# One decay matrix per unit in a chunked DeltaNet layer: the strength moved to the other side of the triangular system, and the second layer-start work held back

## The chip, the core and the metric

The kernel runs on one core of a Trainium2 chip. The core has a matrix engine (TensorE, PE in the profile; its weight loads are PEld), three engines for elementwise work (VectorE, DVE; ScalarE, ACT; GpSimd, POOL) and a queue that issues DMAs (SyncE, SP). Each engine works through its own instructions in order and waits on semaphores for the others. The metric is the time of one execution in microseconds, as a median over several runs.

## The reference

Two layers over a sequence of 1024 tokens and 1024 channels. Layer 0 is a gated DeltaNet (16 value heads, 8 key heads of 128), layer 1 is a softmax attention with a forget bias. Before each layer stands an RMSNorm whose result is scaled and shifted by a projection of a conditioning vector c (adaLN), and the layer's output is multiplied by a gate that comes from the same projection. The change touches layer 0. Its core, cut to what matters:

```python
# per head, per chunk of tokens; g = cumulative log decay inside the chunk
decay = exp(where(lower, g[:, None] - g[None, :], -inf))
kb, vb = k * beta[:, None], v * beta[:, None]
L = where(strict, (kb @ k.T) * decay, 0)
T = inverse(I + L)                      # unit lower triangular
u = T @ vb
w = T @ (kb * exp(g)[:, None])
attn = (q @ k.T) * decay
# scan over the chunks
v_new = u - w @ state
o     = (q * exp(g)[:, None]) @ state + attn @ v_new
state = state * exp(g_last) + (k * exp(g_last - g)[:, None]).T @ v_new
```

q and k are normalised per head (l2norm) after a short causal convolution. The strength beta, and with k unnormalised also the square of the reciprocal norm of k, multiplies the rows of L. The same matrix can be had with the strength as a diagonal on the other side: with B the diagonal of strengths and N the strictly lower part of (k k^T) * decay, (I + B N)^-1 B = B (I + N B)^-1.

## The kernel before

The kernel uses chunks of 128 tokens, two halves of 512 tokens (four chunks each), and units: a unit is one key head with its two value heads in one half, so there are 16 units, 8 per half. Matrix products of the projections run as three products of numbers split in a high and a low part (`mm3`), so each weight tile is cast to `whi` on ACT and its rest `wlo` is taken on DVE (`split`, L323 and L326). In the first half each split tile is written to a cache in HBM (`wc`, L719); in the second half it is read back (`proj_src`, L398).

For each unit run these stages, each of which is a generator:

- `proj_conv`: the projections for k, q and two v tiles, with the convolution on DVE (L743).
- `prepk`: builds a decay matrix `d1` (`decay`, L828 to 854), brings k to token order (`to_tokens`, evicted as `ktok`, L902), takes the reciprocal norm on POOL (`rk`, L867), the strengths `un`, `wn`, `weg`, and multiplies k k^T by strength and decay into `lm` (L884).
- `invert_blocks`: writes the diagonal blocks of `lm` to HBM (`lb`), reads them back spread over partitions (`lr`), inverts the 16 by 16 blocks on DVE (`xi`, L1065 and L1069), writes them (`rb`) and reads them into `rmat` (L1082). `invert_merge` joins blocks on PE with small matmuls (`su`, `tr`), copies on ACT and transposes on DVE (`tmat`).
- `prepv`: brings v to token order (`vtok`, L902) and multiplies it by `un` on POOL (L918).
- `prep2`: builds a second decay matrix `d2`, `qd` = q times exp(g) (L929) and the attention weights `am` (L937).
- `chain`: four steps over the chunks, with `xp` (L957), `vn` on ACT (L970), `ve` on DVE (L971), the state and the outputs `og`.
- `finish`: norm, gate and split of the outputs of both heads, then two DMAs of 512 KB to `og_d` and `ogl_d` (L1037).

A decay matrix starts with `gb`, a 512 KB DMA that spreads two rows of g (in `g_d`, written by `gates`, L696) over all partitions (L834); `affine_select` on POOL writes g with the triangle filled (L840), and eight `exp` on ACT finish it (L852). `gb` has one buffer, `d1` and `d2` have two each. Banks of PSUM are rings: `tr` has two, so a third transpose group waits until the first was evicted.

At the start `start_norm` normalises the first half and computes the scale and shift of layer 0 from eight weight tiles each (accumulated on DVE at L555 for the first six, `KPE`, and on PE with one-column matmuls for the rest). `ada_all` computes everything else of adaLN in 16 strips of 256 columns: 128 DMAs of 128 KB (`oraw`, L265), each followed by one DVE operation (L270, L272). Before its first load it touches the three `oraw` buffers with a copy of `scol[0]` (L1177), so that the loads can't start before that column exists. `next_norm` prepares the second half's input.

What sets the order: the order on PE is written by a planner (`Flow`). Each stage is a generator that yields the time (the `Y_` constants) until its next part is due; the planner always runs the due stage of highest priority, and the projections (later the output projection) are the filler at the lowest. The order on DVE, ACT, POOL and SP is made by the framework's scheduler from dependencies, priorities and its own estimates. So PE never takes a later matmul ahead of one that waits, and SP never issues a later DMA ahead of one that waits.

After layer 0 the output projection (`out_proj_a`) streams its weights twice; then come layer 1 and its output projection, which the change doesn't touch.

Of the kernel before, what the change touches and what calls it, by code (L numbers as in the profile page):

```python
# [37 lines left out]
Y_PK = 1200  # L38
# [4 lines left out]
Y_P2 = 4000  # L43
# [10 lines left out]
Y_F1 = 800  # L54
Y_F2 = 2550
# [25 lines left out]
KPE = 6  # L81
# [100 lines left out]
def tile_trunk(  # L182
# [209 lines left out]
    def proj_src(src, key, again):  # L392
        def load():
            if again:
# [10 lines left out]
            return [(hi, lo, key)]  # L405
# [85 lines left out]
    with ExitStack() as sa:  # L491
# [34 lines left out]
        def start_norm():  # L526
            xsT = [at([P, HALF], n, b) for n, b in (("k", KQ), ("k", KQ), ("k", KQ), ("q", 2), ("q", 2))]
            xsT += [at([P, HALF], "ktok", 3) for _ in range(3)]
            for t in range(CPH):
                xt = at([P, D], *(("vtok", 3), ("qd", 2))[t // 2])  # L530
                nc.sync.dma_start(xt, x[t * P : (t + 1) * P, :])
                for d in norm_tile(xt, at([P, D], "ogt", 1), lambda k, p, t=t: nc.scalar.copy(
                    xsT[k][:, t * P : (t + 1) * P], p)):
                    flow.t += d
            tags = [("d1", 2), ("og", 2), ("zg", ZG), ("d1", 2), ("og", 2), ("zg", ZG), ("gb", 1)]
# [10 lines left out]
            for n in range(2):  # L546
                ps = banks[n]
                acc = at([P, D], "d2", 2)
                for k in range(KT):
# [8 lines left out]
                    for s, c, on in ((acc, ones[:, 0:1], k == KPE), (w, cond[:, k : k + 1], k >= KPE)):  # L558
                        for j in range(KT if on else 0):
                            mm(  # L560
                                ps[:, j : j + 1], s[:, j * P : (j + 1) * P], c,
                                start=s is acc and j == 0, stop=k == KT - 1 and j == KT - 1,
# [29 lines left out]
        def norm_tile(xt, jk, evac):  # L592
            rs = rms_rows(xt, jk, at)
# [13 lines left out]
        def next_norm():  # L607
            yield from hold(lambda: done["kqv"] >= 2)
            for t in range(CPH):
                tok = CPH * P + t * P  # L610
                xt = at([P, D], "nx", 1)
                nc.sync.dma_start(xt, x[tok : tok + P, :])
                yield 4000
                hf = at([P, KT, P], "nh", 1)

                def evac(k, p):
                    nc.vector.tensor_scalar(
                        hf[:, k], p, gcol[0][:, k : k + 1], scol[0][:, k : k + 1],
                        op0=ALU.mult, op1=ALU.add,
                    )  # L620

                yield from norm_tile(xt, hf.rearrange("p k t -> p (k t)"), evac)
                yield 3000
                nc.sync.dma_start(
                    h1_d[:, :, t * P : (t + 1) * P].rearrange("k p t -> p k t"), hf
                )
# [12 lines left out]
        def gates(h, gt):  # L639
# [44 lines left out]
            nc.scalar.activation(ex, ex, AF.Exp)  # L684
            ngc = at([P, CPH, 16], "g_ngc", 2)
# [12 lines left out]
            gt.update(col=col, ex=ex, ngc=ngc, beta=beta, g_d=g_d)  # L698
# [132 lines left out]
        def decay(t, name):  # L831
            gb = at([P, 2, HALF], "gb", 1)
# [5 lines left out]
            dv = at([P, 2 * CPH, P], name, 2)  # L838
            low = name == "d1"
            nc.gpsimd.affine_select(  # L840
                out=dv, in_=gb.rearrange("p j (c t) -> p (j c) t", t=P),
                compare_op=ALU.is_gt if low else ALU.is_ge, fill=BIG if low else -BIG, base=0,
                pattern=[[0, 2 * CPH], [-1 if low else 1, P]], channel_multiplier=1 if low else -1,
            )
            bias = t["gt"]["col" if low else "ngc"]
            yield Y_DG
            for j in range(2):
                for c in range(CPH):
# [4 lines left out]
                        dv[:, u], dv[:, u], AF.Exp, scale=-1.0 if low else 1.0, bias=bias[:, c, hd : hd + 1]  # L853
                    )
            return gb, dv

        def prepk(t):
            g, gt, kf = t["g"], t["gt"], t["k"]
            _, d1v = yield from decay(t, "d1")
            yield Y_PK  # L860
            t["ktok"] = ktok = at([P, CPH, P], "ktok", 3)
            t["ss"] = ss = at([P, 2, CPH], "gss", 3)
            yield from to_tokens(kf, ktok, ss[:, 0])
            yield Y_PS
            rk = at([P, CPH], "rk", 2)
            nc.vector.tensor_scalar(rk, ss[:, 0], EPS, None, op0=ALU.add)
            nc.gpsimd.tensor_tensor(rk, rk, mhalf[:, 0:CPH], op=ALU.pow)  # L867
            rkb = bc(rk, 2, 2)
            t["un"] = un = at([P, CPH, 2], "un", 3)
            t["wn"] = wn = at([P, CPH, 2], "wn", 2)  # L870
            t["weg"] = weg = at([P, CPH, 2], "weg", 3)
            nc.vector.tensor_tensor(un, gt["beta"][:, :, 2 * g : 2 * g + 2], rkb, op=ALU.mult)
            nc.vector.tensor_tensor(wn, un, rkb, op=ALU.mult)
            nc.vector.scalar_tensor_tensor(
# [944 lines left out]
```

## Time and profile before

| what | value |
|---|---|
| median of 3 runs | 2058.69 us (2054.26 to 2058.92) |
| the profiled execution | 2063.72 us, its span 2062.0 us |
| PE, DVE, ACT, POOL busy | 1853.8, 1364.0, 1033.1, 476.4 us |
| instructions | 36440 |
| mean granted TensorE clock | 0.952 |
| DMA | 322.55 MB, 156 GB/s over the span |

The span goes from the first to the last instruction. Busy times of PE are of pipelined matmuls and don't say that PE is at its peak. A row of the waits names who waited, for whom, the total in us, how often, and the longest; a row of the timeline starts with the time in us from the start of the span and the duration, and ends with the number of equal instructions in the row and, in brackets, the idle time ahead and what ended it. In the table of stretches each engine has its busy time in us with the number of instructions, then follow the granted clock, the share of the DMA engines and GB/s.

### The profile page before, as it was taken

What the parts mean: (1) busy time and instruction counts of PE and PEld (TensorE: products, weight loads), DVE (VectorE), ACT (ScalarE), POOL (GpSimd) and SP (SyncE); (2) the same over time, 40 slices, a digit from 0 to 9 for tenths busy, and PEclk for the clock granted to TensorE, in tenths of its full rate; (3) what the DMA queues carried; (4) which work ended last, traced back from release to release, by engine and by line L of the source; (5) the groups of instructions that cost most, each with busy time, mean ns of one, the idle gap of its engine ahead of it and who ended that gap; (6) DMA issues with size and microseconds to landing.
All of it is one profiled execution on the core that took longest, in us unless ns stands there. A gap on an engine that the chain in (4) does not pass through costs nothing.

```text
span 2062.0 us, 36440 instructions
## 1 busy us (share of the span) xinstructions
PE 1853.8 (90%) x12972; PEld 1549.9 (75%) x12972; DVE 1364.0 (66%) x3310; ACT 1033.1 (50%) x2678; POOL 476.4 (23%) x518
## 2 busy tenths in 40 slices
PE   5867898988998889989989788999999999999898
PEld 5655676767776677778778566879889889889676
DVE  5867888778767567665666476537656566666664
ACT  3554565554545345554444343336555565555631
POOL 2021221211213122212101231421231331331222
PEclk7888999999999999999999999999999999999999
DMA  8767676667655545454459998310211110111522
GB/s 320 255 194 219 192 248 205 202 211 238 198 164 178 154 133 176 128 177 140 145 172 311 323 317 274 108 53 27 67 45 33 57 57 32 57 59 40 170 84 95
DMA packets 238166, 322.55 MB, mean 156 GB/s; under 512 B 103896, under 2 KB 156656, under 8 KB 237984
## 3 DMA queue, kind: packets, MB, share of 16 engines
q1 hardware_dynamic: 237984, 320.22, 48.4%
q8 instruction: 102, 1.67, 0.3%
q14 instruction: 80, 0.66, 0.1%
HBM read 235.34 MB, written 84.81 MB: 155 GB/s over the span
## 4 chain that ended last, share of the span: by engine, by line
PE 57%; DMA 16%; DVE 14%; ACT 5%; issue 3%; POOL 3%; SPq 2%; DVEq 0%; POOLq 0%; ACTq 0%
PE mm L127 36%; PE lg L127 5%; PE pt L131 3%; PE oT L127 3%; DMA oraw<-in_ada_w_dram 3%; PE su L127 2%; PE tr L131 2%; PE co L127 2%; DMA rmat<-rb 2%; DVE wlo L326 2%; DMA ohi<-og_d 2%; PE ch L127 2%; DVE cv_y L743 1%; DMA gb<-g_d 1%; DVE xtmp L1065 1%
## 5 line engine op out<-in xcount | busy, mean ns | idle before, releaser
L127 PE MATMUL mm<-ht_h,whi 128*128 128x512 f32 x784 | 352.1, 449 | 8.8 <-DVE olo L299 6.2
L127 PE MATMUL mm<-ht_l,whi 128*128 128x512 f32 x784 | 317.2, 405 | 5.7 <-DVE ht_l L582 5.7
L127 PE MATMUL mm<-ht_h,wlo 128*128 128x512 f32 x784 | 317.5, 405 | 0.9 <-POOL wlo L326 0.9
L127 PE MATMUL mm<-whi,h_h 128*128 128x384 f32 x512 | 187.3, 366 | 1.7 <-ACT whi L323 1.7
L127 PEld LDWEIGHTS mm<-ht_h,whi 128*128 128x128 f32 x784 | 155.0, 198 | 40.3 <-DVE olo L299 6.7
L127 PEld LDWEIGHTS mm<-ht_h,wlo 128*128 128x128 f32 x784 | 153.4, 196 | 37.0 <-POOL wlo L326 1.3
L127 PEld LDWEIGHTS mm<-ht_l,whi 128*128 128x128 f32 x784 | 154.9, 198 | 32.6 <-DVE ht_l L582 6.9
L127 PE MATMUL mm<-wlo,h_h 128*128 128x384 f32 x512 | 174.1, 340 | 2.7 <-POOL wlo L326 2.7
L743 DVE SCALAR_TENSOR_TENSOR cv_y<-cv_t,conv_h,cv_y 128x512 f32<-128x512 f32 x192 | 146.5, 764 | 42.7 <-ACT cv_y L735 40.4
L127 PE MATMUL mm<-whi,h_l 128*128 128x384 f32 x512 | 173.6, 339 | 0.0
L1559 DVE TENSOR_TENSOR ptl<-pt,pth 128x512 fp32r<-128x512 f32 x192 | 106.3, 555 | 85.0 <-ACT pth L1558 83.3
L1558 ACT CAST pth<-pt 128x512 fp32r<-128x512 f32 x192 | 91.3, 477 | 130.5 <-PE pt L131 129.4
L1402 POOL TENSOR_TENSOR rs<-ss,mhalf 128x4 f32<-128x4 f32 x64 | 64.5, 1007 | 313.3 <-DVE ss L1400 310.6
L1523 ACT ACTIVATE lg<-lg,mx 128x896 f32<-128x896 f32 (+7 forms) x128 | 99.5, 777 | 54.1 <-DVE mx L1515 49.8
L326 DVE TENSOR_TENSOR wlo<-ht_h,whi 128x512 fp32r<-128x512 f32 x124 | 92.3, 785 | 49.9 <-ACT whi L323 44.0
L323 ACT CAST whi<-ht_h 128x512 fp32r<-128x512 f32 x124 | 70.5, 619 | 91.4 <-DMA ht_h<-in_wa_o_dram 37.4
L127 PEld LDWEIGHTS mm<-wlo,h_h 128*128 128x128 f32 x512 | 97.9, 191 | 6.3 <-POOL wlo L326 4.4
L127 PEld LDWEIGHTS mm<-whi,h_h 128*128 128x128 f32 x512 | 98.5, 192 | 4.4 <-ACT whi L323 2.0
L127 PE MATMUL mm<-h_h,whi 128*128 128x512 f32 x240 | 100.4, 419 | 0.6 <-DVE wlo L1658 0.3
L131 PE MATMUL pt<-ident,lg 128*128 128x128 f32 (+1 forms) x584 | 96.6, 275 | 2.8 <-ACT lg L1523 2.8
L127 PEld LDWEIGHTS mm<-whi,h_l 128*128 128x128 f32 x512 | 97.2, 190 | 0.0
L127 PE MATMUL mm<-h_h,wlo 128*128 128x512 f32 x240 | 94.8, 395 | 0.0
(356 smaller groups left out, 4660.6 us busy)
## 6 DMA issues: line engine op xcount, KB each, us to landing
ht_h<-in_wa_o_dram SPq DMA_DIRECT2D x62, 512.0 KB
wc<-whi SPq DMA_DIRECT2D x48, 512.0 KB
wc<-wlo SPq DMA_DIRECT2D x48, 512.0 KB
wlo<-wc SPq DMA_DIRECT2D x48, 512.0 KB
whi<-wc SPq DMA_DIRECT2D x48, 512.0 KB
wlo<-in_wa_c_dram SPq DMA_DIRECT2D x32, 512.0 KB
oraw<-in_ada_w_dram SPq DMA_DIRECT2D x128, 128.0 KB
gb<-g_d SPq DMA_DIRECT2D x32, 512.0 KB
```

The costliest lines, as they stand in the source:

```text
L127: self.nc.tensor.matmul(out, lhsT, rhs, start=start, stop=stop)
L131: self.nc.tensor.transpose(out, src, ident)
L323: nc.scalar.copy(hi, src)
L326: (lo_eng or nc.gpsimd).tensor_tensor(lo, src, hi.bitcast(F32), op=ALU.subtract)
L743: nc.vector.scalar_tensor_tensor(y, raw[:, j : j + HALF], w[:, j : j + 1], y, op0=ALU.mult, op1=ALU.add)
L1065: nc.vector.tensor_tensor(tv, bc(lr[:, j + 1 :, j], 1, m), xi[:, 0:m, j : j + 1].broadcast_to([P, m, n]), op=ALU.mult,)
L1402: nc.gpsimd.tensor_tensor(rs, ss, mhalf[:, 0:4], op=ALU.pow)
L1523: nc.scalar.activation(lg, lg, AF.Exp, scale=-1.0, bias=mx[:, hh : hh + 1], accum_out=sums[:, tt : tt + 1],)
L1558: nc.scalar.copy(ph_[:, cs], pp[:, cs])
L1559: nc.vector.tensor_tensor(pl_[:, cs], pp[:, cs], ph_[:, cs].bitcast(F32), op=ALU.subtract)
```

## The change

1. **One decay matrix.** `decay` is called once per unit, in `prepk`, after k was brought to token order; it builds `d2` alone (three buffers instead of two), with `gb` in two buffers instead of one, and also takes the exponential of `gb` that `qd` needs. `prep2` uses `gb` and `d2` as they are. `lm` is now k k^T times strength times `d2` and so the transposed matrix, with the strength on the other index; it has its own tile. The inverse and its merges take the operands in the other order (32 by 16 instead of 16 by 16 in one of the first two products); the first product reads `tmat` and the second `rmat`.
2. **The strength on the other side.** `un` and `weg` are gone. v is scaled by `irk`, the norm of k, when ACT evicts it, two chunks of both heads at a time (POOL's product, L918, is gone), `xp` uses a negated exp(g), and the strength `wn` multiplies the solution: `vn` becomes two ACT operations of 128 columns with a scale instead of one copy of 256, and `ve` multiplies by `wex`.
3. **Held until the gates.** The three copies in `ada_all` and a new one in `next_norm` read `ngc` of the first gates instead of `scol[0]`, so that the strips' loads and the second half's first input wait for the gates.
4. **Start.** `KPE` goes from 6 to 7, and the `gb` tag of `start_norm`'s weight tiles has two buffers.
5. **Cache.** The first three tiles (`KC`) aren't written to the cache; in the second half they are loaded and split again.
6. **Finish and next norm.** `finish` works head by head with one buffer each for `ogt`, `ogh`, `ogl` of 512 columns, and stores with four DMAs of 256 KB; `next_norm` works in halves.
7. Some `Y_` constants of the planner change.

The diff, cut:

```diff
-KPE = 6
+KPE = 7
+KC = 3
...
-            if again:
+            if again and key >= KC:
...
-            tags = [("d1", 2), ("og", 2), ("zg", ZG), ("d1", 2), ("og", 2), ("zg", ZG), ("gb", 1)]
+            tags = [("d1", 2), ("og", 2), ("zg", ZG), ("d1", 2), ("og", 2), ("zg", ZG), ("gb", 2)]
...
                 xt = at([P, D], "nx", 1)
+                if t == 0:
+                    nc.vector.tensor_copy(xt[:, 0:KT], ts[0]["gt"]["ngc"][:, 0, 0:KT])
                 nc.sync.dma_start(xt, x[tok : tok + P, :])
...
-                if k == 2 and key is not None:
+                if k == 2 and key is not None and key >= KC:
...
-        def decay(t, name):
-            gb = at([P, 2, HALF], "gb", 1)
+        def decay(t):
+            gb = at([P, 2, HALF], "gb", 2)
...
-            dv = at([P, 2 * CPH, P], name, 2)
-            low = name == "d1"
+            dv = at([P, 2 * CPH, P], "d2", 3)
...
+            for j in range(2):
+                yield 2 * Y_DX
+                nc.scalar.activation(gb[:, j], gb[:, j], AF.Exp)
             return gb, dv
...
-            _, d1v = yield from decay(t, "d1")
-            yield Y_PK
             t["ktok"] = ktok = at([P, CPH, P], "ktok", 3)
             t["ss"] = ss = at([P, 2, CPH], "gss", 3)
+            yield Y_PT
             yield from to_tokens(kf, ktok, ss[:, 0])
-            yield Y_PS
+            t["gb"], t["d2"] = yield from decay(t)
...
+            nc.vector.tensor_tensor(irk, irk, rk, op=ALU.mult)
...
+            t["lm"] = lm = at([P, 2 * CPH, P], "d1", 2)
...
                     nc.vector.scalar_tensor_tensor(
-                        d1v[:, u], mq[:, c * P : (c + 1) * P], wn[:, c, j : j + 1], d1v[:, u],
+                        lm[:, u], mq[:, c * P : (c + 1) * P], wn[:, c, j : j + 1], t["d2"][:, u],
...
-            for j in range(2):
+            for c0 in range(0, CPH, 2):
                 yield Y_PT
-                yield from to_tokens(vt[:, j], vtok[:, :, j], None)
...
+                    nc.scalar.activation(
+                        vtok[:, c].rearrange("p j f -> p (j f)"), tr[:, o : o + 2 * P], AF.Copy,
+                        scale=t["irk"][:, c : c + 1],
+                    )
...
-            for c in range(CPH):
-                nc.gpsimd.tensor_tensor(vtok[:, c], vtok[:, c], bc(t["un"][:, c], 2, P), op=ALU.mult)
...
-            gb, d2 = yield from decay(t, "d2")
+            gb, d2 = t["gb"], t["d2"]
...
-                nc.scalar.copy(vn, p1[:, 256:512])
+                for j in range(2):
+                    nc.scalar.activation(
+                        vn[:, j * P : (j + 1) * P], p1[:, 256 + j * P : 256 + (j + 1) * P], AF.Copy,
+                        scale=wn[:, c, j : j + 1],
+                    )
...
-            ogh = at([P, 2, HALF], "ogh", 1, F32R)
-            ogl = at([P, 2, HALF], "ogl", 1, F32R)
-            for j in range(2):
-                split(ogh[:, j], ogl[:, j], ogt[:, j], lo_eng=nc.vector)
-                yield 1500
-            for v, d in ((ogh, og_d), (ogl, ogl_d)):
...
+                yield Y_F1
+                ogh, ogl = at([P, HALF], "ogh", 1, F32R), at([P, HALF], "ogl", 1, F32R)
+                split(ogh, ogl, ogt, lo_eng=nc.vector)
+                yield Y_F2
+                for v, d in ((ogh, og_d), (ogl, ogl_d)):
+                    nc.sync.dma_start(d[2 * g + j, :, h * HALF : (h + 1) * HALF], v.bitcast(F32))
...
                 for b in range(4):
-                    o = 32 * b
-                    mm(
-                        pbk[b][o : o + 16, us], lm[sls[b], u, o : o + 16], r[sls[b], u, o + 16 : o + 32],
-                        start=True, stop=True,
-                    )
+                    h16 = slice(32 * b, 32 * b + 16)
+                    mm(pbk[b][sls[b], us], lm[h16, u, sls[b]], tms[b][0:16, u, 0:16], start=True, stop=True)
...
             for _ in range(3):
-                nc.vector.tensor_copy(xt_([P, 2 * P], "oraw", 3)[:, 0:KT], scol[0])
+                nc.vector.tensor_copy(xt_([P, 2 * P], "oraw", 3)[:, 0:KT], ts[0]["gt"]["ngc"][:, 0, 0:KT])
```

**Where it moves instructions.** On SP, at the start of layer 0, around the write of the first gates' g (`g_d`). `oraw` are the strips' weight loads, `wc` the writes to the cache, `wlo` loads of projection weights, `gb` the spread of g. Before:

```order
L265 DMA oraw<-in_ada_w_dram 128x256 x3
L401 DMA wlo<-in_wa_c_dram 128x1024
L265 DMA oraw<-in_ada_w_dram 128x256 x21
L401 DMA wlo<-in_wa_c_dram 128x1024
L265 DMA oraw<-in_ada_w_dram 128x256
```

```order
L696 DMA g_d<-cv_t 16x512
L401 DMA wlo<-in_wa_z_dram 128x1024
L834 DMA gb<-g_d 128x1024
L719 DMA wc_1190<-whi 128x1024
L719 DMA wc_1191<-wlo 128x1024
L834 DMA gb<-g_d 128x1024
L401 DMA wlo<-in_wa_z_dram 128x1024
L719 DMA wc_1253<-whi 128x1024
L719 DMA wc_1254<-wlo 128x1024
L834 DMA gb<-g_d 128x1024 x2
```

and with the change:

```order
L739 DMA wc_1002<-whi 128x1024
L739 DMA wc_1003<-wlo 128x1024
L266 DMA oraw<-in_ada_w_dram 128x256 x3
L716 DMA g_d<-cv_t 16x512
L627 DMA nx<-in_x_dram 128x1024
L402 DMA wlo<-in_wa_z_dram 128x1024
L266 DMA oraw<-in_ada_w_dram 128x256
L854 DMA gb<-g_d 128x1024 x2
L739 DMA wc_1065<-whi 128x1024
L266 DMA oraw<-in_ada_w_dram 128x256 x2
```

Of the strips' 128 loads 35 stood ahead of `g_d`, now 3; the first two units' `gb` now stand next to each other.

On ACT, the first two units. `d_757` and `d_881` are the `d1` of units 0 and 1, `d_872` the `d2` of unit 0; with the change `d_772` and `d_949` are the `d2` of units 0 and 1. Before:

```order
L852 ACTIVATE d_757<-d_757,g_gc 128x128 x8
L898 ACTIVATE sqt,gss<-tr 128x128
L747 ACTIVATE cv_t<-cv_y 128x512
L852 ACTIVATE d_872<-d_872,g_ngc 128x128 x3
L928 ACTIVATE gb<-gb 128x512
L852 ACTIVATE d_872<-d_872,g_ngc 128x128
L928 ACTIVATE gb<-gb 128x512
L852 ACTIVATE d_872<-d_872,g_ngc 128x128 x4
L898 ACTIVATE sqt,gss<-tr 128x128 x2
L902 COPY ktok<-tr 128x512
L898 ACTIVATE sqt,gss<-tr 128x128 x4
L902 COPY vtok<-tr 128x4x128 x2
```

and with the change:

```order
L870 ACTIVATE d_772<-d_772,g_ngc 128x128 x4
L919 ACTIVATE sqt,gss<-tr 128x128
L870 ACTIVATE d_949<-d_949,g_ngc 128x128 x3
L875 ACTIVATE gb<-gb 128x512 x2
L870 ACTIVATE d_949<-d_949,g_ngc 128x128 x5
L767 ACTIVATE cv_t<-cv_y 128x512
L919 ACTIVATE sqt,gss<-tr 128x128 x3
L923 COPY ktok<-tr 128x512
L919 ACTIVATE sqt,gss<-tr 128x128 x4
L940 ACTIVATE vtok<-tr,irk 128x256 x4
```

The eviction `ktok` of unit 0 went ahead of all exponentials; the `ktok` shown is unit 1's, and the first `vtok` now stands behind the exponentials of both units.

On ACT again, the casts `ogh` of one unit's outputs, with the change:

```order
L754 COPY cv_t<-mm 128x512
L755 ACTIVATE cv_y<-mm,conv_h 128x512
L1000 ACTIVATE vn<-ch,wn 128x128 x2
L324 CAST ogh<-ogt 128x512 x2
L1029 ACTIVATE sqt,so<-co 128x128 x2
L1032 COPY og<-co 128x256
```

The second of the two casts writes the buffer that the DMA of the first reads; in the order before the two heads had a buffer each.

More of the change, by code (lines that the diff above doesn't have):

```diff
@@ L37 @@
 Y_PT = 650
-Y_PK = 1200
+Y_PK = 1000
 Y_DG = 2500
@@ L561, in start_norm @@
                                 ps[:, j : j + 1], s[:, j * P : (j + 1) * P], c,
-                                start=s is acc and j == 0, stop=k == KT - 1 and j == KT - 1,
+                                start=s is acc and j == 0, stop=s is w and k == KT - 1 and j == KT - 1,
                             )
@@ L592, in norm_tile @@
         def norm_tile(xt, jk, evac):
-            rs = rms_rows(xt, jk, at)
+            if jk is None:
+                ss = at([P, 2], "ln_s2", 2)
+                for c in range(2):
+                    nc.scalar.activation(
+                        at([P, HALF], "nh", 1), xt[:, c * HALF : c * HALF + HALF], AF.Square,
+                        accum_out=ss[:, c : c + 1],
+                    )
+                nc.vector.tensor_tensor(ss[:, 0:1], ss[:, 0:1], ss[:, 1:2], op=ALU.add)
+                nc.vector.tensor_scalar(ss[:, 0:1], ss[:, 0:1], 1.0 / D, EPS, op0=ALU.mult, op1=ALU.add)
+                rs = at([P, 1], "ln_rs", 2)
+                nc.gpsimd.tensor_tensor(rs, ss[:, 0:1], mhalf[:, 0:1], op=ALU.pow)
+            else:
+                rs = rms_rows(xt, jk, at)
             nc.vector.tensor_scalar(xt, xt, rs, None, op0=ALU.mult)
@@ L697, in gates @@
             done["gates"] = h + 1
-            gt.update(col=col, ex=ex, ngc=ngc, beta=beta, g_d=g_d)
+            gt.update(neg=neg, ex=ex, ngc=ngc, beta=beta, g_d=g_d)
         def z_after(i):
@@ L909, in prepv @@
             vtok = at([P, CPH, 2, P], "vtok", 3)
-            for j in range(2):
+            for c0 in range(0, CPH, 2):
                 yield Y_PT
-                yield from to_tokens(vt[:, j], vtok[:, :, j], None)
+                tr = yield from pst("tr", 2)
+                for c in (c0, c0 + 1):
+                    for j in range(2):
+                        o = (2 * (c - c0) + j) * P
+                        tr_(tr[:, o : o + P], vt[:, j, c], ident)
+                for c in (c0, c0 + 1):
+                    o = 2 * (c - c0) * P
+                    nc.scalar.activation(
+                        vtok[:, c].rearrange("p j f -> p (j f)"), tr[:, o : o + 2 * P], AF.Copy,
+                        scale=t["irk"][:, c : c + 1],
+                    )
+                flow.free(tr, R_T)
             done["tr"] += 1
@@ L969, in chain @@
                 ve = at([P, 2, P], "ve", 2)
-                nc.scalar.copy(vn, p1[:, 256:512])
+                for j in range(2):
+                    nc.scalar.activation(
+                        vn[:, j * P : (j + 1) * P], p1[:, 256 + j * P : 256 + (j + 1) * P], AF.Copy,
+                        scale=wn[:, c, j : j + 1],
+                    )
                 nc.vector.tensor_tensor(
                     ve, p1[:, 256:512].rearrange("p (j f) -> p j f", f=P),
-                    bc(ex[:, 0, c, 2 * g : 2 * g + 2], 2, P), op=ALU.mult,
+                    bc(wex[:, c], 2, P), op=ALU.mult,
                 )
@@ L1164, in invert_merge @@
                 mm(
[L1165 removed]
+                    p3[0:64, u * 64 : u * 64 + 64], pq[64:128, u], r[64:128, u, 64:128],
+                    start=True, stop=True,
                 )
```

103 lines of the change are left out of this document (50 added, 53 removed).

## The prediction

> **What bounds the kernel now.** I read the table of stretches first, cut where the trace changes its character: start, the first units, the first half of layer 0, the change of halves, the second half, the output projection, layer 1.
>
> ```profile
> 0.00:64.00 64.00, 33.72 (x140) 29.89 (x141) 40.03 (x75) 24.91 (x62) 14.35 (x30) 0.66 0.79 281
> 64.00:200.00 136.00, 103.44 (x745) 82.99 (x745) 97.02 (x253) 67.98 (x174) 27.00 (x44) 0.88 0.74 237
> 200.00:600.00 400.00, 357.17 (x3198) 289.24 (x3198) 315.08 (x793) 219.28 (x655) 88.90 (x116) 0.95 0.66 208
> 600.00:700.00 100.00, 81.91 (x549) 67.14 (x547) 66.42 (x179) 45.21 (x140) 22.51 (x29) 0.90 0.54 164
> 700.00:1065.00 365.00, 340.40 (x3133) 279.17 (x3132) 240.30 (x618) 183.08 (x576) 68.16 (x86) 0.98 0.48 144
> 1065.00:1310.00 245.00, 215.46 (x1121) 171.44 (x1120) 151.05 (x261) 102.41 (x216) 54.99 (x38) 0.96 0.88 296
> ```
>
> The columns behind the length are busy us of PE, PEld, DVE, ACT, POOL, then the granted clock. Nearly all of the change lies in the 1001 us from 64 to 1065. PE is busy there for 882.9 us and idle for 118.1; the change hardly alters PE's work, so that idle time, and the 64 us of the start, is what can be won. It isn't even: PE is idle for 32.6 of 136 us among the first units and for 18.1 of 100 at the change of halves, but for 7% of the stretch from 700. The waits of PE from 64 to 1065 name the reasons:
>
> ```profile
> PE su L127 <- DMA rmat<-rb: 22.1, 4, 10.3
> PE tr L131 <- ACT vtok L902: 17.8, 5, 8.5
> PE co L127 <- DVE ve L971: 15.4, 13, 2.9
> PE ch L127 <- DVE xp L957: 14.3, 7, 4.4
> PE tr L131 <- ACT ktok L902: 12.5, 1, 12.5
> PE co L127 <- ACT vn L970: 7.8, 8, 3.0
> PE mm L127 <- DVE olo L299: 6.2, 1, 6.2
> ```
>
> Four single stalls (10.3 on `rmat`, 8.5 on `vtok`, 12.5 on `ktok`, 6.2 on `olo`) make 37.5 us and the other three on `rmat` 11.8; the rest are many short waits inside the chain.
>
> **The change part by part.** All of the sum is made against the profiled execution (2063.72 us, 5.0 over the median of 2058.69) and then taken from the median.
>
> Start. The timeline of PE:
>
> ```profile
> 39.48 3.57 PE L127 MATMUL mm<-ones,d 128*128 128x1 f32 x16 [6.22 <-DVE d L555]
> 52.43 0.80 PE L127 MATMUL mm<-ht_h,whi 128*128 128x512 f32 x1 [2.55 <-ACT ht_h L577]
> 60.55 0.80 PE L127 MATMUL mm<-ht_l,whi 128*128 128x512 f32 x1 [4.18 <-DVE ht_l L582]
> ```
>
> With `KPE` 7 one group of eight one-column products per pass goes, of the form of the first row (-3.5), and DVE does one more accumulation at L555, some 1.3. The strips' loads no longer compete with the last weight tiles, nor do two cache writes and one early x tile of 512 KB each: at the stretch's 281 GB/s these 1.5 MB and the first 0.8 MB of strips are 8 us of DMA, of which I count half as ahead of the last tile (-4). On DVE the strips' operations stand between those that make `ht_l`; without them the 4.18 us go mostly (-3). About **-9**, from -12 to -5.
>
> First stall. The same view of SP, ACT and PE, and of POOL and DVE for later:
>
> ```profile
> 95.76 0.32 SPq L696 DMA_DIRECT2D g_d<-cv_t  x1
> 104.74 0.32 SPq L834 DMA_DIRECT2D gb<-g_d  x1
> 103.26 1.46 POOL L840 TENSOR_SCALAR_AFFINE_SELECT d<-gb 128x1024 f32<-128x1024 f32 x1 [4.13 <-DMA gb<-g_d]
> 110.23 1.10 POOL L840 TENSOR_SCALAR_AFFINE_SELECT d<-gb 128x1024 f32<-128x1024 f32 x1 [4.93 <-DMA gb<-g_d]
> 104.75 2.44 ACT L852 ACTIVATE d<-d,g_gc 128x128 f32<-128x128 f32 x8
> 115.40 0.58 ACT L902 COPY ktok<-tr 128x512 f32<-128x512 f32 x1
> 116.03 1.11 PE L131 MATMUL tr<-ident,vt 128*128 128x128 f32 x4 [12.48 <-ACT ktok L902]
> ```
>
> PE waits for a bank that holds `ktok`, which in ACT's order stands behind the exponentials of two matrices, made from two `gb` loads that share one buffer: the second (5.5 us from issue to POOL) starts after POOL has read the first. From `g_d` to `ktok` pass 20 us. Afterwards the first `ktok` stands ahead of the exponentials, but PE's third transpose group then needs unit 1's `ktok`, which stands behind two units' exponentials. The two loads overlap: 7.5 us to the first matrix on POOL, 2 more for the second load, POOL 1.2, then 16 exponentials at 2.44 for 8 and four of `gb`, taken like the copy of that size at 0.58, make 7.2: 18. So the stall only shrinks: **-2.5** (0 to -12.5).
>
> Second and third stall.
>
> ```profile
> 134.00 0.79 PE L127 MATMUL mm<-ht_h,whi 128*128 128x512 f32 x1 [6.25 <-DVE olo L299]
> 191.25 3.56 DMA rb<-xi
> 194.94 1.78 SPq L1082 DMA_DIRECT2D rmat<-rb  x4
> L1092 DVE STREAM_TRANSPOSE tmat<-rmat 32x256 f32<-32x256 f32 x64 | 27.9, 436 | 30.2 <-DMA rmat<-rb 28.9
> L127 PE MATMUL su<-rmat,d 32*16 32x16 f32 x512 | 11.5, 177 | 22.1 <-DMA rmat<-rb 22.1
> L127 PE MATMUL su<-pp,tmat 32*32 32x32 f32 x512 | 11.7, 196 | 0.0
> ```
>
> (The last three rows are groups of the stretch from 100 to 1100.)
>
> The second is DVE's copy `olo` that stands behind unit 1's work, held up by two further `gb` loads in series; with one load per unit that work is done earlier. **-6** (-6.2 to 0). The third is unit 1's inverse: from `gb` through `lb`, `lr`, DVE, `rb` to `rmat`, all on SP's one queue. In the new order unit 1's `rmat` is 95 DMAs behind `g_d` instead of 89, yet two `gb` loads, each of which holds the queue until POOL has freed the buffer, are gone from between them, and it now comes ahead of unit 2's loads. **-7** of 10.3 (-10.3 to +1.7, the latter since the first merge product now reads `tmat`, four DVE transposes of 0.44 us behind `rmat`). The merges' products change shape from 16 to 32 columns; PE is busy for 11.5 us with 512 records of the one and 11.7 of the other, so that costs nothing.
>
> Change of halves. Here too four loads stand in series (first and last shown); what PE waits for:
>
> ```profile
> 612.22 0.70 SPq L834 DMA_DIRECT2D gb<-g_d  x1
> 636.80 0.32 SPq L834 DMA_DIRECT2D gb<-g_d  x1
> 646.04 0.56 ACT L902 COPY vtok<-tr 128x512 f32<-128x512 f32 x1
> ```
>
> This `vtok` stands behind the exponentials of the fourth load; two overlapping loads end some 17 us sooner. The stall of 8.5 us hangs on it, and unit 9's inverse behind it, which is most of the 11.8 on `rmat`. PE's idle 18.1 us here against 6.7 in 100 us of the next stretch leave 11: **-10** (-20.3 to 0). The six reads from the cache that become three raw loads with six casts help SP and cost ACT 6 casts of 0.6, beside the projections.
>
> Steady part, ACT, POOL, DVE, from the groups of 64 to 1065:
>
> ```profile
> L918 POOL TENSOR_TENSOR vtok<-vtok,un 128x256 f32<-128x256 f32 x64 | 41.7, 682 | 102.5 <-ACT vtok L902 92.2 <-DVE rmat L1167 5.3 <-DVE xtmp L1065 5.0
> L840 POOL TENSOR_SCALAR_AFFINE_SELECT d<-gb 128x1024 f32<-128x1024 f32 x32 | 38.5, 1204 | 131.6 <-PE co L127 58.9 <-DMA gb<-g_d 38.2 <-DMA wlo<-wc 9.4
> L970 ACT COPY vn<-ch 128x256 f32<-128x256 f32 x58 | 21.7, 374 | 36.2 <-PE ch L127 35.9
> L996 ACT ACTIVATE sqt<-co 128x128 bf16<-128x128 f32 x116 | 31.9, 275 | 93.4 <-DVE state L990 62.3 <-DVE xi L1069 7.4 <-PE tr L127 6.5
> L272 DVE SCALAR_TENSOR_TENSOR ohi<-oraw,cond,ohi 128x256 f32<-128x256 f32 x95 | 50.4, 531 | 14.4 <-DMA oraw<-in_ada_w_dram 13.4 <-DVE rk L866 0.2
> ```
>
> ACT loses 128 exponentials at 0.305 (-39), gains 5 on `vtok` (64 of 0.374 for 32 of 0.58), 11 on `vn`, 4 of casts: -19 of its 516 us in the 1001. PE's waits for `vn`, and for `vtok` without the 8.5, are 17.1; **-3** (-12 to 0). POOL loses 41.7 and half of 38.5, 61 us of 207; nothing on PE's path waits for POOL directly, so nothing is counted.
>
> Costs. 32 of the strips' 128 operations move from the start to behind the gates: 17 us of DVE into a stretch where it is idle for 39 of 136: **+2** (0 to +17). `vn` as two operations of the nearest form, 0.275 each, ends 0.18 later, and `ve` starts behind it; PE waited for one or the other 21 times of 64: **+4** (0 to +11). The last is a new wait: the second `ogh` cast writes the buffer that the first one's DMA reads. A store takes about 3.5 us here (the 3.56 of `rb`). In ACT's order the casts are adjacent in 4 units of 16 and have 1 to 8 instructions between them in the others; at ACT's mean of 0.33 us each that leaves 39 us in which ACT stands, with the evictions of PSUM behind it. ACT is idle half of the time anyway: **+6** (0 to +39). The Trainium skill, DMA: Bandwidth & Descriptors, section Latency and other measured facts, gives about 2 us as the fixed cost of a DMA; by that ACT would stand 16 us and the term would be an estimated +2 or +3, the sum 2030. I stay with the slower row.
>
> The sum: -9 - 2.5 - 6 - 7 - 10 - 3 + 2 + 4 + 6 = -25.5, so 2038.2 for the profiled execution and **2033 us** for the median. With all ends at their best it is -73, at their worst +64.
>
> **The rivals.** *More, through DVE.* A pair of DVE's splits takes longer while POOL works:
>
> ```profile
> 103.08 2.18 DVE L326 TENSOR_TENSOR wlo<-wlo,whi 128x512 fp32r<-128x512 f32 x2
> 134.24 1.27 DVE L326 TENSOR_TENSOR wlo<-wlo,whi 128x512 fp32r<-128x512 f32 x2
> ```
>
> The first overlaps the 1.46 us of POOL's select at 103.26 and loses 0.91, 62% of it. At that rate the 61 us that POOL sheds are up to 38 us of DVE, which is busy 719 of the 1001 us. PE's waits for `ve` and `xp` are 29.7 us; if half goes, -15 more: **2018**. The Trainium skill, SBUF — State Buffer, section SBUF: two separate sides, states that GpSimd and a VectorE operation with two SBUF inputs lock each other out of a shared port; by that rule, the trace agrees. Against it: much of POOL's product fell where DVE wasn't next on PE's path.
>
> *Swallowed.* The output projection from 1065 holds the DMA engines at 0.88; if its loads ran at their own pace whatever layer 0 does, all but a tenth of the 25.5 us would come back as idle time of PE beside the 29.5 that it has there: **2056**. Against it: its loads wait for buffers that PE frees, and so move with PE.
>
> *Slower, through the second cast.* Where SP is held up, the first store is issued late. One weight load waits for PE on average 5.5 us (180.9 in 33) in SP's waits:
>
> ```profile
> SPq L398 <- PE mm L127: 180.9, 33, 12.8
> ```
>
> With 5.5 and 3.5 ACT stands 9 us per unit, 144 in all, and in-order evictions behind it; if a third reaches PE, +48 in place of the +6: -31.5 + 48, **2075**. It decides from 2 us of PE per unit on. Against it: in the order before SP mostly waits for ACT at this store, not the other way.
>
> *It doesn't do what it says:* `d2` and `gb` live longer now and could be freed too late, so that the second load waits as before; then the change of halves and the stalls stay and only the start is won: about **2050**, within the forecast's tail.
>
> **How the numbers follow.** The forecast and its tail 0.57 (2018 to 2050), more through DVE 0.14, swallowed 0.13, slower 0.16. A measurement of this kernel can tell about 0.3% from no change, 6.2 us. Faster: 0.56 + 0.14 + 0.02; same: 0.01 + 0.11; slower: 0.16. For 8 in 10 the range reaches from below the second case to short of the slow one: 2006 to 2065.
>
> **What would show it.** Right: the first projection starts some 9 us earlier, no `oraw` load of weight before `g_d`; PE's wait for `olo` and the two long ones for `rmat` are gone or under 4 us, the one for `ktok` or `vtok` near 130 us in the old trace is still there at 8 to 11 us; the stretch of 100 us around the change of halves has PE idle for 7 to 9 us. Wrong: ACT's waits for a DMA of `og_d` above 60 us in total, PE's waits for `vn` and `ve` above 40 us, or a layer 0 that ends earlier while the output projection ends at the same time.

## The result, and the profile after

The changed kernel takes **2113.16 us** (median, 2111.89 to 2120.30), the kernel before 2058.81 beside it: a ratio of 1.0273 (taken over all runs; the medians alone give 1.0264), with a 95% interval of 1.0246 to 1.0301. It is slower by 54 us where 26 us faster was predicted, and outside the range.

The table of stretches of the changed kernel, as shown of before (length; busy us of PE, PEld, DVE, ACT, POOL; granted clock; DMA share; GB/s):

```profile
64.00:200.00 136.00, 102.69 (x717) 81.73 (x715) 109.37 (x283) 64.99 (x170) 25.09 (x34) 0.85 0.75 242
200.00:600.00 400.00, 343.09 (x2874) 280.22 (x2873) 293.59 (x762) 208.31 (x613) 59.94 (x82) 0.91 0.59 187
600.00:700.00 100.00, 87.17 (x640) 69.88 (x640) 71.65 (x181) 49.98 (x151) 18.85 (x20) 0.93 0.51 160
```

From 200 to 600 us PE is idle for 56.9 us instead of 42.8, and the granted clock is 0.91 instead of 0.95. The last product of layer 0's chain (`co`) ends at 1169 us instead of 1130. The waits of PE from 64 to 1120 us say for whom:

```profile
PE tr L132 <- DVE k L770: 47.4, 11, 6.7
PE tr L132 <- ACT ktok L923: 10.4, 1, 10.4
PE tr L128 <- DVE nh L634: 10.3, 2, 8.4
PE co L128 <- DVE ve L1004: 8.1, 8, 4.7
PE ch L128 <- DVE xp L986: 7.8, 4, 3.7
PE co L128 <- ACT vn L1000: 7.7, 5, 5.2
PE mm L128 <- DVE olo L300: 4.3, 1, 4.3
```

The four waits for the DMA of `rmat` and most of those for `vtok` are gone, as intended (`nh` is the second half's input as `next_norm` makes it). The first row is new: PE waits 47.4 us, 11 times, for `k`, the last operation of the convolution (L770), which k's transposes (L132) read. One of the 11, in the timelines of PE, ACT and DVE of the changed kernel (rows of three views, one below the other):

```profile
523.70 0.39 PE L128 MATMUL mm<-ht_l,whi 128*128 128x512 f32 x1
523.92 0.39 PE L128 MATMUL mm<-ht_h,wlo 128*128 128x512 f32 x1
531.00 1.12 PE L132 MATMUL tr<-ident,k 128*128 128x128 f32 x4 [6.69 <-DVE k L770]
```

```profile
521.78 0.58 ACT L754 COPY cv_t<-mm 128x512 f32<-128x512 f32 x1
522.26 0.69 ACT L755 ACTIVATE cv_y<-mm,conv_h 128x512 f32<-128x512 f32 x1
...
528.57 0.63 ACT L767 ACTIVATE cv_t<-cv_y 128x512 f32<-128x512 f32 x1 [1.18 <-DVE cv_y L763]
```

```profile
525.66 0.59 DVE L1023 SCALAR_TENSOR_TENSOR state<-state,g_ex,co 128x128 f32<-128x128 f32 x2
526.17 2.31 DVE L763 SCALAR_TENSOR_TENSOR cv_y<-cv_t,conv_h,cv_y 128x512 f32<-128x512 f32 x3
528.39 1.83 DVE L1120 STREAM_TRANSPOSE tmat<-rmat 32x256 f32<-32x256 f32 x4
530.25 0.69 DVE L770 SCALAR_TENSOR_TENSOR k<-cv_t,cv_y 128x512 f32<-128x512 f32 x1
```

Behind k's last projection product come two ACT operations, three on DVE, one on ACT and one on DVE, 4.9 us without a gap; here they also stand in DVE's order behind other work, and k is made 9 us after ACT began. The new order puts `to_tokens(k)` at the front of `prepk`, due `Y_PT` = 650 units behind the projection. The planner counts a projection product as 215 of these units (0.42 for each of 512 columns), and in the first two rows one follows the other at 0.22 us, so 650 units are some 0.7 us of such products. PE goes through its list in order and stands.

The price isn't only the wait. The granted clock in steps of 2 us around it (PE busy, clock, DMA share, GB/s):

```profile
524.00:526.00 2.00, 0.31 (x2) 1.00 0.92 303
526.00:528.00 2.00, 0.00 (x0) 0.81 1.00 311
528.00:530.00 2.00, 0.00 (x0) 0.50 0.78 247
530.00:532.00 2.00, 1.00 (x5) 0.50 0.25 102
532.00:534.00 2.00, 2.00 (x7) 0.50 0.00 0
534.00:536.00 2.00, 2.00 (x10) 0.98 0.00 0
```

A step that begins at 1, ends at 0.5 and has 0.81 in the mean puts the fall near 527.2, some 3 us after PE's last product (524.3); the clock comes back only after another 3 us of work. The Trainium skill, TensorE: Matmul & The Clock Gate, section Part 1: The HAM clock gate, states that an idle window of about 3.4 us halves PE's clock and about 3.4 us of sustained work restore it; these rows agree but for some tenths of a us. In the 2 us behind the end of each of the ten waits of 3.0 us and more the granted clock is 0.50 eight times, 0.56 once and 1.00 once; two of the ten rows, behind a wait of 5.3 us and behind the shortest:

```profile
967.90:969.90 2.00, 2.00 (x7) 0.50 0.00 0
846.60:848.60 2.00, 2.00 (x13) 1.00 0.03 8
```

### The profile page after: what moved, and what is told of

The parts are those of the page before. It is cut to its first block, busy times and chain, and to the rows that moved or that the text cites. A ratio compares the mean times of both kernels' runs of the same rounds, so it can differ in the third digit from the quotient of the medians.

```text
span 2110.1 us, 36328 instructions
## 1 busy us (share of the span) xinstructions
PE 1874.3 (89%) x12940; PEld 1564.5 (74%) x12940; DVE 1358.8 (64%) x3341; ACT 1029.7 (49%) x2660; POOL 418.4 (20%) x438
## 4 chain that ended last, share of the span: by engine, by line
PE 57%; DVE 15%; DMA 14%; ACT 6%; issue 5%; POOL 2%; SPq 2%; DVEq 0%; POOLq 0%; ACTq 0%
PE mm L128 36%; PE lg L128 5%; PE pt L132 3%; PE oT L128 3%; DMA oraw<-in_ada_w_dram 3%; PE tr L132 3%; DVE cv_y L763 3%; PE su L128 3%; PE co L128 2%; PE ch L128 2%; DVE wlo L327 2%; DMA wraw<-in_wb_dram 2%; DVE d L905 1%; DMA ohi<-og_d 1%; ACT whi L324 1%
## 5 line engine op out<-in xcount | busy, mean ns | idle before, releaser
L324 ACT CAST whi<-wlo 128x512 fp32r<-128x512 f32 (+1 forms) x108 | 62.4, 626 | 86.8 <-PE mm L128 62.1
L132 PE MATMUL pt<-ident,lg 128*128 128x128 f32 (+1 forms) x584 | 96.4, 275 | 2.3 <-ACT lg L1551 2.3
```

Of the source, the lines that this page charges most:

```text
L132: self.nc.tensor.transpose(out, src, ident)
L324: nc.scalar.copy(hi, src)
```

## The experiments

Theories A to G are named in the texts on record where they first appear; the main question is A, k's early transposes, against B, that the loss lies elsewhere and PE would find the same delay under another name. All ratios are to the kernel before, run beside each.

| kernel | median us | before beside it | ratio, 95% interval |
|---|---|---|---|
| e1_k_later | 2048.49 | 2056.24 | 0.9968, 0.9947 to 0.9989 |
| e1_k_behind_decay | 2055.24 | 2056.24 | 0.9992, 0.9973 to 1.0012 |
| e5_before_k_first | 2089.71 | 2056.24 | 1.0158, 1.0132 to 1.0183 |
| e3_before_hold | 2058.77 | 2056.24 | 1.0004, 0.9988 to 1.0019 |
| e6_filled_wait | 2106.13 | 2056.45 | 1.0247, 1.0218 to 1.0277 |
| e4_before_finish | 2057.13 | 2056.45 | 1.0006, 0.9987 to 1.0024 |
| e7_before_vn_two | 2056.21 | 2056.45 | 0.9998, 0.9985 to 1.0011 |
| e9_later_strips | 2040.44 | 2056.45 | 0.9936, 0.9910 to 0.9962 |
| e11_3000 | 2070.15 | 2059.47 | 1.0061, 1.0035 to 1.0086 |
| e10_9000 | 2034.29 | 2059.47 | 0.9871, 0.9838 to 0.9904 |
| e12_no_hold | 2047.59 | 2059.47 | 0.9941, 0.9919 to 0.9963 |
| e14_kpe6 | 2044.85 | 2059.47 | 0.9936, 0.9911 to 0.9961 |

**k's transposes later (e1_k_later).** The changed kernel with one number changed:

```diff
-            yield Y_PT
+            yield 6000
             yield from to_tokens(kf, ktok, ss[:, 0])
```

> The changed kernel, with k's transposes due 6000 instead of 650 of the planner's units behind k's last projection matmul. Theory A (PE reaches k's transposes before DVE has finished the convolution that makes k: 47.4 us of waits in the changed kernel's trace): PE's wait for k at L770 falls from 47.4 to under 10 us and the time from 2113 to 2065 to 2085. Theory B (the loss lies in the stalls of the second half's input, of the two-part vn and of the casts of the outputs; PE finds the same delay elsewhere): the wait for k falls too, but the time stays between 2100 and 2120.

2048.49 us: the whole loss is gone and 0.3% is won over the kernel before. PE's waits in it, and the page's busy times (first of the changed kernel, then of this one):

```profile
PE co L128 <- DVE ve L1004: 19.1, 13, 4.5
PE tr L132 <- ACT vtok L940: 19.0, 8, 4.2
PE su L128 <- DVE tmat L1120: 12.6, 2, 12.3
PE tr L132 <- ACT ktok L923: 11.2, 1, 11.2
...
PE tr L132 <- DVE k L770: 0.6, 1, 0.6
```

```profile
PE 1874.3 (89%) x12940; PEld 1564.5 (74%) x12940; DVE 1358.8 (64%) x3341; ACT 1029.7 (49%) x2660; POOL 418.4 (20%) x438
```

```profile
PE 1850.6 (91%) x12940; PEld 1543.4 (76%) x12940; DVE 1353.3 (66%) x3341; ACT 1029.1 (50%) x2660; POOL 414.8 (20%) x438
```

The spans, 2110.1 and 2043.5 us, differ by 66.6: PE is idle for 235.8 and 192.9 us, 42.9 of it, and is busy for 23.7 us longer with the same 12940 products. The second part is slower work, at a granted clock of 0.953 instead of 0.964. These are one execution of each kernel; the mean clock over all runs is 0.951 (four runs) and 0.958 (eight), nearer to each other, so 23.7 us is at the high end of what the clock can have cost. Theory A holds, and its forecast of the gain had been too small.

**k behind the decay matrix (e1_k_behind_decay).**

```diff
-            yield Y_PT
-            yield from to_tokens(kf, ktok, ss[:, 0])
             t["gb"], t["d2"] = yield from decay(t)
+            yield Y_PK
+            yield from to_tokens(kf, ktok, ss[:, 0])
+            yield Y_PS
```

> The changed kernel, with k brought to token order behind the decay matrix again, as in the kernel before; all other parts of the change stay. Theory A: PE's wait for k falls from 47.4 us to the 0 of the kernel before, and the time to 2065 to 2085; the stall for ktok near 100 us may grow by some us, since ktok stands behind exponentials again. Theory B: 2100 to 2120.

2055.24: the wait for k doesn't occur, the time is that of before. With the later due time alone the place in `prepk` stayed as in the change, so it is the delay that cures it. Whether the way round behind the decay also gives something up isn't shown: this interval and that of e1_k_later overlap.

**Only the early k in the kernel before (e5_before_k_first).**

```diff
-            _, d1v = yield from decay(t, "d1")
-            yield Y_PK
+            yield Y_PT
             yield from to_tokens(kf, ktok, ss[:, 0])
-            yield Y_PS
+            _, d1v = yield from decay(t, "d1")
```

> The kernel before, with only one thing of the change: k is brought to token order ahead of the first decay matrix. Theory A: PE waits 35 to 50 us for k at the convolution's last operation, and the time rises from 2059 to 2085 to 2105, 10 us of the rise given back where the first ktok no longer stands behind 16 exponentials. Theory B: within 10 us of 2059.

33 us slower, with this row among PE's waits:

```profile
PE tr L131 <- DVE k L750: 41.6, 9, 9.2
```

B falls: the one move makes the kernel before slow by itself. It isn't the whole 63 us between the changed kernel and e1 (1.0273 less 0.9968). In this kernel PE's waits for `rmat` (22.1 us before) went away at the same time, while the 10 us that the forecast gave back at the first `ktok` didn't come: that wait is 12.3 us. What makes up the rest isn't shown.

**Half the lateness (e11_3000).** As e1, with 3000 in place of 6000.

> The changed kernel with k's transposes due 3000 units behind the projection (650 in the change: 2113 us and waits of 47.4 us for k; 6000: 2048 us and 0.6 us). Theory A: the ten waits of 3.0 to 6.7 us shrink by 2.3 us each, to about 22 us in all. With theory D (waits over some 3.5 us cost more than their own length, since PE is slower for some us behind them) most of the 23.7 us by which PE is busier in the changed kernel than with 6000 goes too: PE busy 1850 to 1858 us and 2068 to 2080. Without it PE stays busy for over 1865 us and the time is 2085 to 2095.

2070.15. PE's wait for k:

```profile
PE tr L132 <- DVE k L770: 24.5, 10, 3.8
```

The dose counts: ten waits of 3.8 us at most and 24.5 us in all cost 19 us by the ratios (1.0061 less 0.9968), the 47.4 us of the changed kernel cost 63; each of these two costs is known to some 7 us. PE busy is 1853.5 us, hardly above e1's 1850.6, as theory D forecast, but in an execution of 2061.37 us, the fastest of ten. Theory D's limit of 3.5 us doesn't show in it: behind waits of 3.8 and 3.3 us the four transposes take 0.63 us, behind waits of 2.2 and 1.7 us 1.11 us, and there the granted clock is 0.50 and 0.51 (just ahead of the first PE has also waited 1.8 us for `ve`):

```profile
453.85 1.11 PE L132 MATMUL tr<-ident,k 128*128 128x128 f32 x4 [2.22 <-DVE k L770]
```

So the length of a wait alone doesn't decide whether PE is slow behind it.

**The wait filled (e6_filled_wait).** Nothing is left out; the added products are overwritten.

```diff
             tr = yield from pst("tr", 2)
+            for _ in range(fill):
+                nc.tensor.matmul(tr[:, 0:P], ones, ones, start=True, stop=True)
...
-            yield from to_tokens(kf, ktok, ss[:, 0])
+            yield from to_tokens(kf, ktok, ss[:, 0], 12 if g >= 3 else 0)
```

> The changed kernel with the early transposes left as they are, but in the units 3 to 7 and 11 to 15 (those in which PE waits for k) PE works through 12 products of ones with ones ahead of the transposes, into the bank that the transposes then overwrite. That is about 3.5 us of PE by the 0.29 us of a transpose of the same size, so the waits of 3.0 to 6.7 us shrink to at most about 3.2. k isn't ready any sooner. Theory D (a wait of over some 3.5 us also costs afterwards: in the changed trace the granted clock is 0.50 from 528 to 534 us, the last 2 us of a wait and the first 4 us behind it, and PE is busy for 1874 us against 1851 in the kernel with the later transposes): with the clock kept up the time falls from 2113 to 2090 to 2102, although PE has more to do. Theory E (a wait costs only its own length): 2110 to 2118, since nothing comes earlier.

2106.13, between D and E, and its interval overlaps that of the changed kernel. The profile says more than the time (k's transposes of the changed kernel, then of this one, last):

```profile
PE tr L132 <- DVE k L770: 19.2, 11, 4.6
...
L915 PE MATMUL tr<-ones 128*128 128x128 f32 x240 | 28.4, 275 | 0.0
```

```profile
PE 1892.4 (90%) x13180; PEld 1582.6 (75%) x13180; DVE 1361.1 (64%) x3341; ACT 1029.1 (49%) x2660; POOL 417.9 (20%) x438
```

```profile
L132 PE MATMUL tr<-ident,k 128*128 128x128 f32 x64 | 14.1, 361 | 47.4 <-DVE k L770 47.4
L132 PE MATMUL tr<-ident,k 128*128 128x128 f32 x64 | 10.3, 283 | 19.7 <-DVE k L770 19.2 <-ACT rmat L1146 0.5
```

With the wait filled a transpose of k takes 283 ns in the mean instead of 361; with the later due time (e1) it takes 284. So it is PE's idling that slows the products behind the wait. Filler and rest of the wait make 47.6 us, as before, but without the 28.4 us of filler PE is busy for 1864.0 us, 10 less than in the changed kernel. The time fell by 7 (5 by the ratios), which the noise can make; the profiled execution, of 2113.17 us, is the slowest of four. By an estimate from the changed kernel's rows the same comes out: some 3 us of work at half the clock lose 1.5 us, behind nine waits some 14 of the 23.7 us. That all of it has this cause isn't shown.

**Only the hold, and all but the hold (e3_before_hold, e12_no_hold).** The three copies for `oraw` in the kernel before read `ngc`:

```diff
-                nc.vector.tensor_copy(xt_([P, 2 * P], "oraw", 3)[:, 0:KT], scol[0])
+                nc.vector.tensor_copy(xt_([P, 2 * P], "oraw", 3)[:, 0:KT], ts[0]["gt"]["ngc"][:, 0, 0:KT])
```

> The kernel before, with only the three copies of the strips reading the first gates' ngc instead of the first scale, so that the strips of the second modulation begin behind the gates. As in the prediction (the start -4 to -12, 32 operations of DVE moved behind the gates +0 to +17): 2045 to 2060, the first projection 3 to 9 us earlier. Theory C (the strips fall on DVE where the first two units are made, and hold up k, xi and the merges): 2065 to 2080, with PE's waits for DVE from 64 to 400 us grown by over 10 us.

No difference that can be measured. The first product with `ht_l` starts 3.7 us earlier (56.86 us instead of 60.55), as forecast, and theory C's slowdown doesn't come. But PE's wait of 10.3 us for the second unit's inverse has become one of 15 us for the first unit's, where the kernel before had none:

```profile
166.55 0.21 PE L127 MATMUL su<-rmat,d 32*16 32x16 f32 x2 [15.05 <-DMA rmat<-rb]
```

The reverse edit in e1 (copies back on `scol[0]`, none in `next_norm`):

> The changed kernel with k's transposes due 6000 units behind the projection and with the strips and the second half's input not held until the gates, as before the change. By the prediction the hold wins 9 us at the start and costs 2 later, so without it 2052 to 2060 instead of 2048. By the run of the kernel before with only the hold (2058.8 against 2056.2) it wins nothing: 2044 to 2052, with the start 8 us later and the waits for tmat and ve near 154 and 225 us gone.

2047.59, like e1: the hold wins nothing there either. The first `ht_l` product comes 5.6 us later (57.85 us instead of 52.23). Of the waits that were to go, the 12.3 us for `tmat` became 6.5 us for `nh`, and the 4.5 us for `ve` stayed.

**The held work later still (e9_later_strips).** e1, and:

```diff
-            yield from hold(lambda: done["gates"] == 1)
+            yield from hold(lambda: done["merge"] >= 2)
             for _ in range(3):
-                nc.vector.tensor_copy(xt_([P, 2 * P], "oraw", 3)[:, 0:KT], ts[0]["gt"]["ngc"][:, 0, 0:KT])
+                nc.vector.tensor_copy(xt_([P, 2 * P], "oraw", 3)[:, 0:KT], ts[1]["r"][:, 0, 0:KT])
```

and the same two edits in `next_norm`.

> The changed kernel with k's transposes due 6000 units behind the projection (2048 us alone), and with the strips and the second half's input held until the second unit's inverse is merged, near 220 us, instead of until the gates, near 90 us. Theory F (in the first 200 us the held work falls on DVE and SP among the first two inverses and makes PE's waits of 12.3 us for tmat, 4.8 for vt and 4.5 for ve): those shrink to under 6 us together and the time falls to 2030 to 2042. Theory G (the work is only moved into the stretch from 200 to 600 us, where DVE is busy for 314 of 400 us, and is paid there): 2044 to 2056.

2040.44. From 64 to 200 us PE is busy for 111.9 us (102.9 in e1, 103.4 before):

```profile
64.00:200.00 136.00, 111.88 (x922) 90.00 (x920) 94.31 (x249) 75.23 (x200) 17.83 (x35) 0.91 0.67 217
```

The wait of 12.3 us for `tmat` is gone; PE's waits for `tmat` (L1120), `vt` and `ve` from 64 to 260 us make 7.4 us instead of 22.9, a little over the forecast 6. The time is the one that theory F forecast; by the ratios 7 us of the 9 won there remain (0.9968 less 0.9936), but the intervals of e1 and e9 overlap a little. A part is only moved, as G said: at 268 us PE now waits 6.4 us for `nh`, which it doesn't in e1.

**The casts of the outputs and the two-part `vn` (e4_before_finish, e7_before_vn_two).** The kernel before with the new `finish` (as in the change's diff), and with

```diff
-                nc.scalar.copy(vn, p1[:, 256:512])
+                for j in range(2):
+                    nc.scalar.activation(
+                        vn[:, j * P : (j + 1) * P], p1[:, 256 + j * P : 256 + (j + 1) * P], AF.Copy, scale=1.0
+                    )
```

> The kernel before, with only the new finish: head by head, one buffer each for the cast outputs of 512 columns, four stores of 256 KB. By the prediction's term +6 (0 to +39): 2059 to 2066, with ACT's wait for the store of the first cast at 5 to 40 us. By its rival, in which a third of 144 us reaches PE: 2095 to 2107. If the changed trace's 9.9 us of that wait is typical and ACT has the time: within 4 us of 2057.

> The kernel before, with only vn made by two operations of 128 columns instead of one of 256 (scale 1, so the values are the same). By the prediction's term +4 (0 to +11): 2058 to 2068, PE's waits for vn and ve 23 us before, now 25 to 35. If the two operations are mostly hidden in the chain's slack: within 4 us of 2057.

Neither moves the time. ACT does wait in e4 for the first cast's store, 16.6 us in all, and PE doesn't wait longer for ACT (40.8 us from 64 to 1120 us, 48.1 before). In e7 PE's waits for `vn` and `ve` are 25.0 us, 23.2 before.

```profile
ACT ogh L323 <- DMA og_d<-ogh: 16.6, 6, 4.3
```

**Two sizes (e10_9000, e14_kpe6).** e9 with 9000 in place of 6000, and e9 with `KPE` 6.

> The kernel with the later strips (2040 us) with k's transposes due 9000 instead of 6000 units behind the projection. If k's lateness for PE ends near 6000: within 5 us of 2040, since the inverse that begins with k has room. If each unit of delay is paid in the inverse: 16 units by 3 us, of which a third reaches PE, 2050 to 2060.

2034.29: there is room beyond 6000, and this version is 1.3% faster than before and 3.9% faster than the change (0.9871 over 1.0273). By the ratios it is 13 us faster than e9, more than either forecast, and only in part for k's sake: e9 still waits 4.9 us for k, e10 not at all. Where the rest of the 13 us comes from isn't shown. The kernel before wasn't fitted in the same way, so the 1.3% isn't the worth of the change alone.

> The kernel with the later strips (2040 us) with KPE 6 instead of 7: two more groups of one-column products on PE at 3.5 us each pass, and one operation less on DVE, 1.3 us, in each of the two passes, behind which PE waits for 9.1 us. The prediction counted the step to 7 as -3.5 with +1.3, so 2041 to 2045 here. If the wait for DVE at 29 us decides: 2036 to 2040.

The same ratio as e9, 0.9936: the 3.5 us of products that PE saves with 7 come back as its longer wait for DVE's accumulation (9.1 us with 7, 5.6 with 6).

## Why the prediction was wrong, point by point

**The step that failed** is one that has no term. The prediction priced the move of `to_tokens(k)` as a gain on ACT ("Afterwards the first `ktok` stands ahead of the exponentials") and never asked when its input is ready. The trace of before had the answer; ACT's and DVE's rows of one k there:

```profile
378.86 0.58 ACT L734 COPY cv_t<-mm 128x512 f32<-128x512 f32 x1
...
379.84 0.71 ACT L735 ACTIVATE cv_y<-mm,conv_h 128x512 f32<-128x512 f32 x1
...
383.10 0.63 ACT L747 ACTIVATE cv_t<-cv_y 128x512 f32<-128x512 f32 x1 [1.19 <-DVE cv_y L743]
```

```profile
380.65 2.33 DVE L743 SCALAR_TENSOR_TENSOR cv_y<-cv_t,conv_h,cv_y 128x512 f32<-128x512 f32 x3 [0.38 <-ACT qq L1108]
...
383.76 0.69 DVE L750 SCALAR_TENSOR_TENSOR k<-cv_t,cv_y 128x512 f32<-128x512 f32 x1 [0.44 <-ACT cv_t L747]
```

5.6 us from the first to the end of the last, against 0.7 that the new due time leaves: some 5 us for a unit in which little else stands between on PE. The trace after has ten such waits in 16 units; ten times 5 us, an estimate, would have given +50 in the sum and so the right sign. For the rest of the 63 us the slower work behind the waits is the likeliest, shown in part (e6).

**The other terms**, against the runs without that fault:

- Start, -9: right at its place. The first product with `ht_l` begins at 52.89 us instead of 60.55 (-7.7). But it isn't worth 9 us at the end: the hold alone makes the start 3.7 us earlier and the ratio 1.0004 (e3), and `KPE` 7 instead of 6 wins nothing (e14). So the "+2 (0 to +17)" for the strips behind the gates was too small, if the hold's start is worth what it shows there; the runs don't price the strips apart.

```profile
52.89 0.80 PE L128 MATMUL mm<-ht_l,whi 128*128 128x512 f32 x1 [3.42 <-DVE ht_l L583]
```

- First stall (`ktok`), -2.5: 12.5 became 10.4. Right. It lies near 97 us; the prediction's "near 130 us" was wrong, its own rows have it at 104 to 116.
- Second stall (`olo`), -6: 6.2 became 4.3, and 0.8 in e1. Right in kind.
- Third stall (`rmat`), -7: the named wait went, but another of 8.4 us for `nh` (12.3 for `tmat` in e1) stands near 155 us, one unit earlier. The prediction followed the second unit's inverse through SP's queue and not the first one's through DVE, where held strips and the second half's input now stand. e9 takes that wait away, with 6.4 us for `nh` at a later place.
- Change of halves, -10: in e1 PE is idle there for 8.5 instead of 18.1 us. Right; in the changed kernel itself, where the stretch is shifted, for 12.8.

```profile
600.00:700.00 100.00, 91.48 (x667) 74.11 (x666) 70.71 (x192) 51.83 (x151) 15.10 (x21) 0.97 0.59 184
```

- ACT, -3 by a relief of 19 us: ACT's busy time fell by 3.4 over the span. The sizes were those of operations with a constant scale; one with a scale for each partition takes longer (the last section's rows). PE's waits for `vtok` in e1, 19.0 us, are what they were.
- `vn`, +4, and the casts, +6: both 0 (e7 with a constant scale, so without the longer operation, and e4). In the changed kernel PE's waits for `ve` and `vn` fell from 23.2 to 15.8 us; in e1 they are 22.2.

The sum without the missing term was -25.5; e1 measured -8 and e12 -12. The start with its cost (-9 and +2 in the sum; hold and `KPE`, its two measured parts, 0) and the third stall (-7, shifted rather than removed) would close most of that gap; they weren't measured apart inside e1.

**The rivals.** "Slower, through the second cast" had the sign and not the place: ACT waits 9.9 us for it in the changed kernel, not 144. "More, through DVE": POOL is busy for 418.4 us instead of 476.4, as forecast, and DVE's most frequent large operation doesn't get faster (before, then after):

```profile
L743 DVE SCALAR_TENSOR_TENSOR cv_y<-cv_t,conv_h,cv_y 128x512 f32<-128x512 f32 x192 | 146.5, 764 | 42.7 <-ACT cv_y L735 40.4 <-ACT qq L1108 0.4
```

```profile
L763 DVE SCALAR_TENSOR_TENSOR cv_y<-cv_t,conv_h,cv_y 128x512 f32<-128x512 f32 x189 | 147.5, 780 | 39.0 <-ACT cv_y L755 36.7
```

"Swallowed": from the changed kernel to e1 the chain of layer 0 ends 57 us earlier (1169 to 1112) and the span is 67 shorter, so what is won in layer 0 arrives. "It doesn't do what it says": the stalls that it named are smaller or gone; it does.

## What to carry to other kernels

When a step is moved ahead in an in-order list, read from the trace when its input is ready, operation by operation, before counting what its output releases; a due time that was harmless behind another stage is a stall for every unit in front of it. A kernel whose order is planned by constants should be compared with the constants fitted to it: here one number cost 63 us and hid that the rest won 8. And look at the first unit of a pipeline, not only at the one that waits now, when work is moved in among the first ones.

## What the runs showed of the hardware

**Behind a wait PE can work at half its clock.** Nine of the ten waits of 3.0 to 6.7 us in the changed kernel were followed by work at a granted clock of 0.50 to 0.56, and k's transposes took 361 ns instead of 284; 47.4 us of waits cost 63. In e11 two waits of 2.2 and 1.7 us were followed by it too and two of 3.8 and 3.3 us weren't, so these runs give no length from which on it happens. Nor is a wait for k the only cause of a low clock: from 200 to 600 us it is 0.91 in the changed kernel, 0.94 in e1, e6 and e11, and 0.90 in e10, whose profile shows 1865.4 us of PE.

**On ACT, a scale for each partition is dearer than a constant one.** The copy of 256 columns before, two of 128 with scale 1 (e7), and with the column `wn` (e1):

```profile
L970 ACT COPY vn<-ch 128x256 f32<-128x256 f32 x58 | 21.7, 374 | 36.2 <-PE ch L127 35.9
```

```profile
L971 ACT ACTIVATE vn<-ch 128x128 f32<-128x128 f32 x118 | 26.4, 279 | 34.1 <-PE ch L127 33.8
```

```profile
L1000 ACT ACTIVATE vn<-ch,wn 128x128 f32<-128x128 f32 x120 | 37.5, 365 | 46.3 <-PE ch L128 40.7 <-DVE xtmp L1093 5.2
```

279 ns became 365: 86 ns more, so half the width takes as long as the whole did. The Trainium skill, ScalarE: Activation LUTs, section What ACT_TABLE_LOAD costs, gives about 93 ns for each operand that is one value per partition; the rows agree.
